# A two-layer hybrid decoder trunk: gate projections placed between attention heads, zero-padded low parts, softmax sums folded into the RMS norm, and scaling moved to ScalarE

## The chip, the cores and the metric

The kernel runs on one core of one Trainium2 chip. The metric is the device time of one execution in microseconds. Smaller is better. Times before and after are medians of several executions; the trace comes from one further execution under the hardware profiler.

## The reference

Two layers, each x <- LayerNorm(alpha * x + f(x)) three times: a hybrid token mixer, a cross-attention into 256 memory tokens, and a dense SwiGLU network. There are 512 tokens of width 1024. The change touches the mixer, cut here to what matters:

```python
def diff_attention(q, k, v, lam, subln_g, lambda_init):        # branch A: 4 heads, 2 softmaxes each
    s = einsum('bqhcd,bkhcd->bhcqk', q, k) * HEAD_DIM ** -0.5
    p = softmax(where(causal, s, -inf))
    w = p[:, :, 0] - lam * p[:, :, 1]
    o = einsum('bhqk,bkhe->bqhe', w, v)
    return rms_norm(o, subln_g) * (1.0 - lambda_init)
...
def rg_lru_branch(xr, gate, ...):                              # branch B: recurrence
    xc = causal_conv(xr)
    gates = einsum('bsnc,gncd->gbsnd', blocks_of_64(xc), gate_w) + gate_b
    ...                                                        # h_t = a_t * h_{t-1} + u_t
    return h * gelu(gate)
...
def hybrid_mixer(x, ...):
    aq, ak, av, rx, rg, cq, ck, cv, gl = split(x @ w_in)
    o_a = diff_attention(rotary(aq), rotary(ak), av, ...)
    o_b = rg_lru_branch(rx, rg, ...)
    o_c = dilated_attention(rotary(cq), rotary(ck), cv)        # branch C: 8 heads, band masks
    g = sigmoid(gl.reshape(B, S, 3, D_MODEL))
    return (g[0] * (o_a @ w_br_a) + g[1] * (o_b @ w_br_b) + g[2] * (o_c @ w_br_c)) @ w_out
```

## The kernel before

All data is float32; every large product is made from a rounded high part and a low remainder (`xh`, `xl` of the activations, `whi`, `wlo` of the weights) as three matmuls: high times high, low times high, high times low. The weights come as 372 chunks of 128 x 1024. A chunk is loaded by a DMA of the SP queue (`raw`), ScalarE casts it to `whi` (line 264), and VectorE subtracts to get `wlo` (line 271); for the chunks in `on_pool` GpSimd subtracts.

`make_program` writes a list of *steps*. A step is one 128 x 512 output in PSUM from eight contraction tiles, hence 24 matmuls (lines 808 to 810, or 837 to 839 where weights are the moving side); steps of the branch projections have half of that. The list's order is the order of the matmuls on TensorE. Before each step the loop at the end of the kernel splits weight chunks ahead (at most `pairs` pairs that have still to be used), issues the work that follows the step before (`POST`), and calls `advance()`. That function moves every running *item* on by one stage and starts one waiting item. An item is a Python generator: `attn_a` and `attn_c` (one head or pair of heads, one block of 128 queries), `rope_item` (the rotary embedding of a projected tile), `b_item` (one tile of 128 channels of the recurrence). What an item issues on TensorE in `advance()` thus stands between two steps, in program order, and a TensorE instruction that has to wait holds up the steps behind it. Every engine works through its instructions in program order.

In branch A a head has a Q tile and a K tile, each one step, followed by `rope_item`: ScalarE copies the PSUM tile, VectorE shuffles it, GpSimd does two multiplications with the tables, VectorE adds (line 572), ScalarE makes the high parts (lines 573 and 574); one advance later VectorE makes the low parts, for Q into the tile `ql` (lines 581 and 582, each twice, so that both halves of the 128 partitions hold both heads' remainders), for K into `qkA` itself (585, 586). `attn_a` then makes scores `sc` (336, 337), a masked minimum on VectorE (346), exponentials on ScalarE with their sums (349), the two weightings (352 to 355), transposes `tp` (360) and the product with V (366), an RMS norm with a power on GpSimd (372), and the output's transpose. `attn_c` is alike, with two heads side by side: the probabilities are scaled by the reciprocal sums on VectorE (398), transposed (404) and multiplied with V (410). In `b_item` the tiles `xs` and `xl` are the high and low parts of the convolved input, `xl` from four subtractions on VectorE (516 and 517); the gate products `z` (521, 522) read them, and ScalarE takes four `tanh` from `z` (524 to 527).

All 128 x 512 tiles in PSUM share eight banks. The tiles of 4 KB per partition, among them `raw`, `whi`, `wlo`, `ql` and `xl`, share a pool of 42 (`a4`). The order in layer 1 is: V of branch A, the Q and K tiles of four heads in a row, V of branch C, the eight gate projections of branch A, the first pair of heads of branch C, and so on. In layer 0 V of branch A stands after the second head.

## Time and profile before

| | before |
|---|---|
| median of 3 runs | 2237.24 us (2236.24 to 2237.97) |
| the profiled execution | 2235.22 us |
| its span, first to last instruction | 2233.4 us |
| TensorE busy (matmuls) | 2180.9 us, 98% |
| VectorE busy | 1318.1 us, 59% |
| ScalarE busy | 893.2 us, 40% |
| GpSimd busy | 300.9 us, 13% |
| mean granted TensorE clock | 0.993 |

The span is what the trace covers; the profiled execution is 1.8 us longer than its span. Busy time of TensorE counts matmuls at whatever clock is granted, so a stretch at half clock is busy and yet slow. The difference of span and TensorE's busy time, 52.5 us, is the time in which TensorE did nothing.

### The profile page before, as it was taken

The page shows a single profiled execution, that of the slowest core. Times are in us where ns is not written, and L with a number is a line of the kernel's source. Part 1 is how long each engine was busy: PE and PEld are TensorE (multiplying, and loading weights), DVE is VectorE, ACT ScalarE, POOL GpSimd, SP SyncE. Part 2 cuts the span into 40 slices and gives each one's busy share as a digit, 9 for nine tenths or more (in the row PEclk, how much of TensorE's full clock was granted, in tenths as well). Part 3 has the DMA queues.
Part 4 walks back from the last instruction along what each step waited for, and adds up shares of the span by engine and source line. Part 5 has one row for each costly group of instructions (what it writes and reads, how often), then busy time and mean ns, then how long its engine had stood idle before and what let it go on. Part 6 is the DMA issues. An engine that isn't in the chain of part 4 may idle for free.

```text
span 2233.4 us, 26831 instructions
## 1 busy us (share of the span) xinstructions
PE 2180.9 (98%) x10516; PEld 1812.8 (81%) x10516; DVE 1318.1 (59%) x2154; ACT 893.2 (40%) x1583; POOL 300.9 (13%) x206
## 2 busy tenths in 40 slices
PE   9999989999999999999998999899999999999998
PEld 7788868888888888888876888688888888888887
DVE  7757767756745743244567577678567457432435
ACT  4454557643333323133134445666433333231330
POOL 2203102210300300000022031022103003000000
PEclk9999999999999999999999999999999999999999
DMA  7122223244333322233221222232334233223321
GB/s 269 49 94 77 93 66 112 84 130 146 123 101 107 105 76 85 92 125 110 88 97 54 77 85 91 67 113 95 125 134 132 95 104 104 85 76 113 105 94 38
DMA packets 65278, 224.37 MB, mean 100 GB/s; under 512 B 7936, under 2 KB 7936, under 8 KB 65152
## 3 DMA queue, kind: packets, MB, share of 16 engines
q1 hardware_dynamic: 65152, 222.66, 30.6%
q8 instruction: 83, 1.36, 0.2%
q14 instruction: 43, 0.35, 0.0%
HBM read 212.14 MB, written 2.10 MB: 96 GB/s over the span
## 4 chain that ended last, share of the span: by engine, by line
PE 69%; issue 17%; DVE 7%; ACT 3%; POOL 3%; DMA 0%; SPq 0%; POOLq 0%; ACTq 0%; DVEq 0%
PE ps L808 17%; PE ps L809 17%; PE ps L810 17%; PE ps L837 5%; PE ps L838 5%; PE ps L839 5%; POOL wlo L271 2%; PE o L410 1%; PE o L366 1%; DVE x L478 1%; POOL ln L473 1%; ACT whi L264 1%; DVE ql L582 1%; DVE xl L516 1%; PE sc L337 1%
## 5 line engine op out<-in xcount | busy, mean ns | idle before, releaser
L808 PE MATMUL ps<-xh,whi 128*128 128x512 f32 (+1 forms) x1792 | 690.5, 385 | 4.2 <-ACT ti L527 2.8
L809 PE MATMUL ps<-xl,whi 128*128 128x512 f32 (+1 forms) x1792 | 688.1, 384 | 1.1 <-DVE xl L752 0.5
L810 PE MATMUL ps<-xh,wlo 128*128 128x512 f32 (+1 forms) x1792 | 687.4, 384 | 1.3 <-POOL wlo L271 1.3
L271 DVE TENSOR_TENSOR wlo<-raw,whi 128x1024 fp32r<-128x1024 f32 x347 | 441.9, 1287 | 40.3 <-ACT whi L264 36.5
L264 ACT CAST whi<-raw 128x1024 fp32r<-128x1024 f32 x371 | 382.0, 1045 | 123.8 <-PE ps L838 61.8
L808 PEld LDWEIGHTS ps<-xh,whi 128*128 128x128 f32 x1792 | 339.0, 189 | 72.4 <-ACT ti L527 4.1
L810 PEld LDWEIGHTS ps<-xh,wlo 128*128 128x128 f32 x1792 | 338.9, 189 | 68.5 <-POOL wlo L271 2.1
L809 PEld LDWEIGHTS ps<-xl,whi 128*128 128x128 f32 x1792 | 339.2, 189 | 66.4 <-DVE xl L867 1.1
L473 POOL TENSOR_TENSOR ln<-ln,expo 128x1 f32<-128x1 f32 x24 | 34.4, 1432 | 1081.3 <-DVE ln L472 1081.3
L837 PE MATMUL ps<-whi,hh 128*128 128x512 f32 x352 | 137.1, 389 | 0.0
L839 PE MATMUL ps<-whi,hl 128*128 128x512 f32 x352 | 137.0, 389 | 0.0
L838 PE MATMUL ps<-wlo,hh 128*128 128x512 f32 x352 | 136.9, 389 | 0.0
L497 ACT CAST xh<-tp 128x256 fp32r<-128x256 f32 x80 | 28.0, 376 | 198.6 <-PE tp L491 121.4
L742 ACT CAST hh<-fg 128x512 fp32r<-128x512 f32 x44 | 27.3, 620 | 191.9 <-DVE fg L741 191.9
L731 DVE SCALAR_TENSOR_TENSOR fg<-fg,ps 128x512 f32<-128x512 f32 x44 | 30.3, 688 | 116.8 <-ACT fg L730 116.8
L741 DVE TENSOR_TENSOR fg<-fg,ps 128x512 f32<-128x512 f32 x44 | 30.2, 687 | 114.4 <-PE ps L810 114.4
L730 ACT ACTIVATE fg<-ps 128x512 f32<-128x512 f32 x44 | 26.3, 598 | 140.7 <-PE ps L810 140.7
L678 DVE SCALAR_TENSOR_TENSOR x<-ps,x 128x512 f32<-128x512 f32 x48 | 32.9, 686 | 80.5 <-PE ps L839 80.4
L839 PEld LDWEIGHTS ps<-whi,hl 128*128 128x128 f32 x352 | 66.1, 188 | 13.7
L838 PEld LDWEIGHTS ps<-wlo,hh 128*128 128x128 f32 x352 | 66.1, 188 | 13.7
L837 PEld LDWEIGHTS ps<-whi,hh 128*128 128x128 f32 x352 | 66.1, 188 | 13.6
L567 POOL TENSOR_TENSOR raw<-raw,tabs 128x512 f32<-128x512 f32 x32 | 42.8, 1339 | 242.5 <-ACT raw L564 242.5
(233 smaller groups left out, 3555.7 us busy)
## 6 DMA issues: line engine op xcount, KB each, us to landing
raw<-in_wts_dram SPq DMA_DIRECT2D x371, 512.0 KB, 3.7
xs<-xs SPq DMA_DIRECT2D x32, 128.0 KB, 2.2
lng<-in_lnp_in_dram SPq DMA_DIRECT2D x6, 512.0 KB, 4.0
lnb<-in_lnp_in_dram SPq DMA_DIRECT2D x6, 512.0 KB, 4.9
tabs<-in_tabs_in_dram SPq DMA_DIRECT2D x4, 512.0 KB, 7.7
x<-in_x_in_dram SPq DMA_DIRECT2D x4, 512.0 KB, 8.5
qkA<-qkA SPq DMA_DIRECT2D x16, 128.0 KB, 2.2
qkC<-qkC SPq DMA_DIRECT2D x16, 128.0 KB, 2.2
```

The costliest lines, as they stand in the source:

```text
L264: A.copy(h, raw)
L271: eng.tensor_tensor(lw, raw, f(h), ALU.subtract)
L473: G.tensor_tensor(st[:, 15:16], st[:, 14:15], expo, ALU.pow)
L567: G.tensor_tensor(raw, raw, tab[:, 0, :], ALU.mult)
L678: V.scalar_tensor_tensor(xs, ps, co, xs, ALU.mult, ALU.add)
L731: V.scalar_tensor_tensor(g, g, 1.0, ps, ALU.add, ALU.mult)
L808: T.matmul(pv, wh, xh, start=(kt == 0), stop=False)
L809: T.matmul(pv, wh, xl, start=False, stop=False)
L810: T.matmul(pv, wl, xh, start=False, stop=(kt == st.nk - 1))
L837: T.matmul(ps, xh, wh, start=(i == 0), stop=False)
L838: T.matmul(ps, xh, wl, start=False, stop=False)
L839: T.matmul(ps, xl, wh, start=False, stop=(i == n - 1))
```

## The change

Five edits. (1) In `make_program` the gate projections of branch A move: in layer 0 from behind V of branch C to places behind the second, third and fourth head (two, three, three), in layer 1 two behind every head; V of branch C follows them. `pairs` of the heads falls from 6 to 5 or 4, that of V of branch C from 6 to 5. (2) `ql` and `xl` are no longer allocated. Three fixed tiles `pad` are zeroed once by GpSimd and used in turn; only the half that carries a head's (or block's) own remainder is written, and the other half stays zero. So two subtractions stand where four did; in `b_item` one of the two goes to GpSimd. The pool `a4` has 39 tiles in place of 42. (3) In `attn_a` the first softmax is not divided by its sum: the second is scaled by -lambda times the ratio of the sums, one full-width multiplication goes, and the square of the first sum times the epsilon takes the epsilon's place in the RMS norm. (4) In `attn_c` the two scalings by reciprocal sums move from VectorE to ScalarE. (5) The first two chunks of the memory's key projection leave `on_pool`, so VectorE makes their low parts.

```diff
+NPAD = 3
...
-        def a_heads(h0, h1):
-            for h in range(h0, h1):
-                tile_step("w_in", l, OFF_AQ + P * h, "x", ("rope", l, "A", h, 0), pairs=6)
-                tile_step("w_in", l, OFF_AK + P * h, "x", ("rope", l, "A", h, 1), pairs=6)
-
-        if l == 0:
-            a_heads(0, 2)
-            group("w_in", l, 0, KT, OFF_AV, "x", ("v", l, "A"), 6)
-            a_heads(2, 4)
-        else:
-            group("w_in", l, 0, KT, OFF_AV, "x", ("v", l, "A"), 6,
-                  needs=("x%d_3_{t}" % (l - 1),), pre=("tabs",))
-            a_heads(0, 4)
+        def a_head(h, pairs):
+            tile_step("w_in", l, OFF_AQ + P * h, "x", ("rope", l, "A", h, 0), pairs=pairs)
+            tile_step("w_in", l, OFF_AK + P * h, "x", ("rope", l, "A", h, 1), pairs=pairs)
...
-        group("w_in", l, 0, KT, OFF_CV, "x", ("v", l, "C"), 6)
-        gates("A", *range(KT))
+        if l == 0:
+            a_head(0, 6)
+            a_head(1, 6)
+            group("w_in", l, 0, KT, OFF_AV, "x", ("v", l, "A"), 6)
+            gates("A", 0, 1)
+            a_head(2, 4)
+            gates("A", 2, 3, 4)
+            a_head(3, 4)
+            gates("A", 5, 6, 7)
+        else:
+            group("w_in", l, 0, KT, OFF_AV, "x", ("v", l, "A"), 6,
+                  needs=("x%d_3_{t}" % (l - 1),), pre=("tabs",))
+            for h in range(4):
+                a_head(h, 5 if h < 2 else 4)
+                gates("A", 2 * h, 2 * h + 1)
+        group("w_in", l, 0, KT, OFF_CV, "x", ("v", l, "C"), 5)
...
-        return big.tile([P] + shape, dt, tag="a4", name=nm(s), bufs=42)
+        return big.tile([P] + shape, dt, tag="a4", name=nm(s), bufs=39)
...
+    pads = [cp.tile([P, 2, S], F32R, tag="pad%d" % k, name="pad%d" % k) for k in range(NPAD)]
+    turn = [0]
+
+    def padded():
+
+        turn[0] += 1
+        return pads[turn[0] % NPAD]
...
-               if (name == "xkv" and c0 < D) or (name == "w_up" and c0 % HID < 2 * P)}
+               if (name == "xkv" and 2 * P <= c0 < D) or (name == "w_up" and c0 % HID < 2 * P)}
...
-        V.reciprocal(st[:, 4:6], st[:, 2:4])
-        V.tensor_scalar(st[:, 6:7], st[:, 5:6], neglam[:, l:l + 1], None, ALU.mult)
-        V.tensor_scalar(pr[0][:, :w], pr[0][:, :w], st[:, 4:5], None, ALU.mult)
+        V.reciprocal(st[:, 4:5], st[:, 3:4])
+        V.scalar_tensor_tensor(st[:, 6:7], st[:, 2:3], neglam[:, l:l + 1], st[:, 4:5], ALU.mult, ALU.mult)
         V.scalar_tensor_tensor(pr[0][:, :w], pr[1][:, :w], st[:, 6:7], pr[0][:, :w],
                                ALU.mult, ALU.add)
+        V.tensor_scalar(st[:, 5:6], st[:, 2:3], st[:, 2:3], LN_EPS, ALU.mult, ALU.mult)
...
-        V.tensor_scalar(st[:, 8:9], st[:, 7:8], LN_EPS, None, ALU.add)
+        V.tensor_tensor(st[:, 8:9], st[:, 7:8], st[:, 5:6], ALU.add)
...
-            V.tensor_scalar(pr[c][:, :w], pr[c][:, :w], st[:, 4 + c:5 + c], None, ALU.mult)
+            A.activation(pr[c][:, :w], pr[c][:, :w], AF.Copy, scale=st[:, 4 + c:5 + c])
...
-        xl = a4("xl", [2, S], F32R)
-        for r in (u, w):
-            V.tensor_tensor(xl[r, 0, :], xc[u], f(xs[u, 0, :]), ALU.subtract)
-            V.tensor_tensor(xl[r, 1, :], xc[w], f(xs[w, 1, :]), ALU.subtract)
+        xl = padded()
+        G.tensor_tensor(xl[u, 0, :], xc[u], f(xs[u, 0, :]), ALU.subtract)
+        V.tensor_tensor(xl[w, 1, :], xc[w], f(xs[w, 1, :]), ALU.subtract)
...
-            ql = a4("ql", [2, S], F32R)
-            for w in (a, b):
-                V.tensor_tensor(ql[w, 0, :], raw[a], f(st[a, 0, :]), ALU.subtract)
-                V.tensor_tensor(ql[w, 1, :], raw[b], f(st[b, 1, :]), ALU.subtract)
+            ql = padded()
+            V.tensor_tensor(ql[a, 0, :], raw[a], f(st[a, 0, :]), ALU.subtract)
+            V.tensor_tensor(ql[b, 1, :], raw[b], f(st[b, 1, :]), ALU.subtract)
...
+    for pd in pads:
+        G.memset(f(pd[64:P, 0, :]), 0.0)
+        G.memset(f(pd[0:64, 1, :]), 0.0)
     make_identity(nc, ident)
```

How instructions stand on three engines before and now. First VectorE in the branch-A heads of layer 1: before, from the Q tile of head 2 on (`ql` is the low part, `sc` the scores of head 0's first query block, `sh` the shuffle of a projected tile; the pair 581, 582 stands twice):

```order
L565 STREAM_SHUFFLE sh_9161<-ps_9129 128x512
L581 TENSOR_TENSOR ql_9168<-raw_9065,qkA_9125 64x512
L582 TENSOR_TENSOR ql_9168<-raw_9065,qkA_9125 64x512
...
L572 TENSOR_TENSOR raw_9113<-raw_9113,sh_9114 128x512
L346 ISA pr_9178,st_9177<-sc_9180,tabs_8779 128x128
...
L271 TENSOR_TENSOR wlo_9158<-raw_9060,whi_9157 128x1024
L565 STREAM_SHUFFLE sh_9222<-ps_9190 128x512
L585 TENSOR_TENSOR qkA_9173<-raw_9113,qkA_9173 64x512
L586 TENSOR_TENSOR qkA_9173<-raw_9113,qkA_9173 64x512
L352 RECIPROCAL st_9177<-st_9177 128x2
```

The same place now, from the low part of head 0's Q tile to the weighting of its first block; `sh_9091` belongs to head 1:

```order
L592 TENSOR_TENSOR pad_80<-raw_8939,qkA_8985 64x512
L593 TENSOR_TENSOR pad_80<-raw_8939,qkA_8985 64x512
L584 TENSOR_TENSOR raw_8979<-raw_8979,sh_8980 128x512
L596 TENSOR_TENSOR qkA_9023<-raw_8979,qkA_9023 64x512
L597 TENSOR_TENSOR qkA_9023<-raw_8979,qkA_9023 64x512
L577 STREAM_SHUFFLE sh_9091<-ps_9059 128x512
L359 ISA pr_9097,st_9096<-sc_9099,tabs_8740 128x128
...
L284 TENSOR_TENSOR wlo_9085<-raw_8972,whi_9084 128x1024
```

Before, the first scores of head 0 stand behind the low parts of head 1's Q tile, while the tiles of head 2 already come out; now they stand behind the shuffle of head 1's Q tile, and no other head's low parts lie between.

Second, ScalarE where the first gate products `z` of the recurrence meet the last head pairs of branch C. Before (`gq` is the GELU of the gate, `tr` and `ti` the four `tanh` of `z`):

```order
L405 COPY wT_2636<-tp_2641 128x256
L661 ACTIVATE gq_2550<-gq_2550 128x512
L393 ACTIVATE pr_2659,st_2658<-pr_2659,st_2658 128x512
L393 ACTIVATE pr_2660,st_2658<-pr_2660,st_2658 128x512
L264 CAST whi_2699<-raw_2545 128x1024
L414 CAST oCh_1797<-o_2707 128x128
L524 ACTIVATE tr_2720<-z_561_2714,hb 64x512
```

Now:

```order
L418 COPY wT_2621<-tp_2626 128x256
L411 ACTIVATE pr_2565<-pr_2565,st_2564 128x384
L411 ACTIVATE pr_2566<-pr_2566,st_2564 128x384
L672 ACTIVATE gq_2535<-gq_2535 128x512
L406 ACTIVATE pr_2641,st_2640<-pr_2641,st_2640 128x512
L406 ACTIVATE pr_2642,st_2640<-pr_2642,st_2640 128x512
L277 CAST whi_2681<-raw_2530 128x1024
L427 CAST oCh_1791<-o_2689 128x128
L536 ACTIVATE tr_2702<-z_552_2696,hb 64x512
```

The two scalings by the reciprocal sums (line 411) have come in ahead of the GELU's `tanh`; the order of the rest is the same.

Third, GpSimd in the last blocks of the recurrence in layer 0. Now (`acc` is the merge of branch C, `bl` the low part of branch B's output, `pad` the low part of a convolved tile):

```order
L559 TENSOR_TENSOR ti_3646<-ti_3646,m_3518 128x512
L640 TENSOR_TENSOR acc_2213<-acc_2213,g_3594 128x512 x2
L569 TENSOR_TENSOR bl_3337<-m_3518,bh_3336 128x512 x2
L528 TENSOR_TENSOR pad_79<-xc_3803,xs_3868 64x512
L559 TENSOR_TENSOR ti_3817<-ti_3817,m_3862 128x512
```

Before, the same five places held the same instructions without the fourth: a low part that VectorE made is now queued on GpSimd behind two merges and two subtractions. On TensorE the instructions between the steps stand as before, item by item; only the steps that they stand between have changed places.

## Rows read from the trace of the kernel before

**Rows 1.** The page: busy time by engine; weight loads (KB, us to landing).

```profile
PE 2180.9 (98%) x10516; PEld 1812.8 (81%) x10516; DVE 1318.1 (59%) x2154; ACT 893.2 (40%) x1583; POOL 300.9 (13%) x206
...
raw<-in_wts_dram SPq DMA_DIRECT2D x371, 512.0 KB, 3.7
```

**Rows 2.** Waits of TensorE over the whole span: total us, times, longest.

```profile
PE tp L360 <- DVE pr L355: 14.3, 6, 5.6
PE sc L336 <- ACT ti L525: 7.1, 4, 2.9
...
PE ps L808 <- ACT ti L527: 2.8, 4, 0.7
PE tp L404 <- DVE st L390: 2.4, 2, 1.2
PE z L522 <- DVE xl L516: 1.6, 2, 0.8
```

**Rows 3.** Busy time in stretches: length, then PE, PEld, DVE, ACT, POOL, clock.

```profile
40.00:60.00 20.00, 20.00 (x90) 16.57 (x89) 12.41 (x15) 10.01 (x14) 2.98 (x2) 1.00 0.53 171
60.00:100.00 40.00, 35.92 (x170) 30.01 (x168) 32.90 (x66) 16.47 (x39) 13.92 (x10) 0.96 0.14 40
280.00:340.00 60.00, 53.79 (x277) 41.75 (x276) 39.00 (x83) 36.37 (x76) 2.91 (x2) 0.94 0.26 73
1160.00:1220.00 60.00, 47.83 (x215) 38.85 (x214) 45.93 (x92) 24.92 (x57) 17.75 (x13) 0.94 0.17 49
1400.00:1440.00 40.00, 33.80 (x173) 25.98 (x172) 28.80 (x62) 22.92 (x49) 1.54 (x1) 0.91 0.23 67
```

**Rows 4.** Stretches with a lower granted clock: length, PE busy, clock.

```profile
90.00:94.00 4.00, 3.50 (x12) 0.57 0.20 48
294.00:304.00 10.00, 6.99 (x20) 0.66 0.00 0
1182.00:1190.00 8.00, 5.91 (x16) 0.57 0.42 115
1408.00:1416.00 8.00, 5.07 (x14) 0.57 0.01 2
```

**Rows 5.** Groups by line: busy us, mean ns, idle time ahead.

```profile
L271 DVE TENSOR_TENSOR wlo<-raw,whi 128x1024 fp32r<-128x1024 f32 x347 | 441.9, 1287 | 40.3 <-ACT whi L264 36.5 <-PE ps L838 3.7
...
L398 DVE TENSOR_SCALAR pr<-pr,st 128x128 f32<-128x128 f32 (+3 forms) x64 | 32.5, 550 | 1.1
...
L516 DVE TENSOR_TENSOR xl<-xc,xs 64x512 fp32r<-64x512 f32 x32 | 27.7, 865 | 0.6 <-ACT xs L509 0.3
...
L405 ACT COPY wT<-tp 128x128 f32<-128x128 f32 (+3 forms) x64 | 24.1, 430 | 1.8 <-PE tp L404 1.7
...
L582 DVE TENSOR_TENSOR ql<-raw,qkA 64x512 fp32r<-64x512 f32 x16 | 15.0, 937 | 0.2
...
L354 DVE TENSOR_SCALAR pr<-pr,st 128x128 f32<-128x128 f32 (+3 forms) x32 | 14.0, 437 | 0.0
...
L772 POOL TENSOR_TENSOR gw<-gr,gw 64x512 fp32r<-64x512 f32 x8 | 11.2, 1404 | 40.9 <-ACT gw L770 40.4
```

**Rows 6.** VectorE at the first gate products of layer 0, in time order.

```profile
284.95 1.52 DVE L516 TENSOR_TENSOR xl<-xc,xs 64x512 fp32r<-64x512 f32 x1
286.49 1.69 DVE L517 TENSOR_TENSOR xl<-xc,xs 64x512 fp32r<-64x512 f32 x1
...
289.83 0.75 DVE L398 TENSOR_SCALAR pr<-pr,st 128x384 f32<-128x384 f32 x2
```

**Rows 7.** ScalarE in the same stretch.

```profile
291.67 0.63 ACT L661 ACTIVATE gq<-gq 128x512 f32<-128x512 f32 x1 [6.41 <-DVE gq L660]
```

**Rows 8.** ScalarE in branch A of layer 1.

```profile
1184.72 0.62 ACT L573 CAST qkA<-raw 64x512 fp32r<-64x512 f32 x1 [5.26 <-DVE raw L572]
```

**Rows 9.** GpSimd at the last gate products of layer 0.

```profile
447.42 3.42 POOL L557 TENSOR_TENSOR bl<-m,bh 128x512 fp32r<-128x512 f32 x2
```

**Rows 10.** TensorE at the same place.

```profile
451.45 0.50 PE L522 MATMUL z<-xl,gw 128*128 128x512 f32 x1 [0.80 <-DVE xl L516]
```

## The prediction

> **What bounds the kernel now.** I read the busy line of the page first: TensorE is busy for 2180.9 of the 2233.4 us of the span, the others for 59% and less [rows 1]. The order lists show TensorE's instructions unchanged, with steps that have changed places, so the change can take away or add only two things: time in which TensorE stands still, 2233.4 - 2180.9 = 52.5 us in all, and time in which it works at a lower clock. Whether VectorE or ScalarE gets lighter counts only where TensorE waits for it.
>
> The waits of TensorE over the whole span say where [rows 2]. The transposes `tp` of branch A wait for VectorE's weighting `pr`, 14.3 us in six waits. Scores `sc` and step outputs `ps` wait for a `tanh` that ScalarE reads out of `z`, 7.1 and 2.8 us: not for its data, but for the PSUM bank that `z` holds. Transposes of branch C wait 2.4 us for a maximum in `st`, and `z` waits 1.6 us for `xl`.
>
> Four stretches hold nearly all of this. Length less PE busy [rows 3]: the A heads of layer 0, 40.00 - 35.92 = 4.08 us; the A heads of layer 1, 60.00 - 47.83 = 12.17; the place where the recurrence's first gate products meet branch C, 60.00 - 53.79 = 6.21 in layer 0 and 40.00 - 33.80 = 6.20 in layer 1. Together 28.66 us. An undisturbed stretch beside them has 90 matmuls in 20.00 us, no idle time and clock 1.00, so 0.222 us a matmul and 5.33 us a step of 24.
>
> Each of the four is followed by a piece at a low granted clock, the lower of the levels 1.2 and 2.4 GHz in part of it [rows 4]. Work at clock c costs (1 - c) of its busy time: 3.50 x 0.43 = 1.5 us, 6.99 x 0.34 = 2.4, 5.91 x 0.43 = 2.5, 5.07 x 0.43 = 2.2, together 8.6. In each, TensorE had stood still before the clock fell.
>
> **The change part by part.** *Gates between heads, half the `ql` work, one weighting fewer* (edits 1, 2, 3). In layer 1, eight rope steps stand in a row. VectorE is busy for 45.93 of 60 us there [rows 3], and the ping-pong between engines adds to it: ScalarE stands 5.26 us for a VectorE sum before it can make a high part [rows 8]. The sequence falls 12.17 us behind over four heads, 3.0 each. Per head the change removes two `ql` subtractions of 0.94, 1.9 us, and one weighting of 0.44 per block, 4 x 0.44 = 1.8, against small one-column operations that I take at 0.2 per block, so 0.8 [rows 5]; net 2.9, nearly the shortfall. Two gate steps per head then give 2 x 5.33 = 10.7 us of TensorE's work that asks of VectorE only two `wlo` of 1.29, so 8.1 us in which it catches up. 2.9 + 8.1 is well over 3.0. In layer 0 the shortfall is 4.08 and there are two or three gates to a head. So I take these waits as gone: 4.08 + 12.17 = 16.25, and their clock losses 1.5 + 2.5 = 4.0; 20.3 us in all. From below: if a wait is pure latency, the gates don't help unless they stand between a block's scores and its transposes; items advance one stage per step, so they do stand there.
>
> *Half the `xl` work, scalings on ScalarE* (edits 2, 4). At the junction VectorE makes four `xl`, from 284.95 on, the first two at 1.52 and 1.69 us, then scales `pr` twice, 0.75 [rows 6]. ScalarE meanwhile waits 6.41 us for the VectorE product behind them, `gq` [rows 7], and its `tanh`, which free the banks, come late. Now VectorE has one `xl` of some 1.7 and no scaling, so ScalarE goes on some 3.6 us earlier; the scalings fill time in which it stood still. TensorE loses its 1.2 us wait for `st` and so reaches the scores 1.2 earlier; of the longest bank wait of 2.9 there remains 2.9 + 1.2 - 3.6 = 0.5. The bank wait of a step, 0.7, and some 1.3 at the next block stay: 2.5 us in each layer, 5.0 together, of 6.21 + 6.20 = 12.41. With no wait over a microsecond the clock should hold, which gives 2.4 + 2.2 = 4.6. Gain 12.41 - 5.0 + 4.6 = 12.0.
>
> *Half of `xl` on GpSimd* (edit 2). The nearest row, GpSimd on 64x512, has 1.40 us, VectorE's `xl` 0.87 [rows 5]. At the last gate products of layer 0 GpSimd makes `bl` from 447.42 to 450.84 [rows 9], and the new half stands behind it: done at 450.84 + 1.4 = 452.2. `z` started at 451.45 after 0.80 of waiting [rows 10], so it may be up to 0.8 late. I take the waits for `xl`, 1.6, as unchanged. For this choice of engine the Trainium skill, GPSIMD Engine Reference, section 4.1 (Engine selection), recommends VectorE for elementwise work on a tile and gives GpSimd as about two times slower for two inputs. Our rows, 1.40 against 0.87, agree in direction; by the page's ratio the half would take an estimated 1.7, and end 0.3 later. What that would do at every block is a rival below.
>
> *At nothing.* ScalarE's 64 scalings: between 0.43, the copy of `wT`, and 0.63, the `gq` of 128x512 [rows 5, 7], so 27.5 to 40 us on an engine that is 40% busy; hidden by its waits, except at the junction, where two at 0.63 would give back 1.3 per layer, or 2.6. Edit 5 gives VectorE four `wlo` more (two per layer), 4 x 1.29 = 5.2 us; no wait for VectorE among the large ones [rows 2] lies at that projection, so work of steps without a wait covers them, and without that cover they cost at most those 5.2. The pool of 39 for 42: `ql` and `xl`, up to two or three at a time, no longer draw on it; a chunk needs 3.7 us to land [rows 1], a cast, and 1.29 for `wlo`, some 6 us, and the pairs ahead reach over at least two steps, over 10 us. If it did not suffice in one group, a chunk's `wlo` would be late by one 1.29. The pads are zeroed in six instructions of at most 1.4 us, 8.4 us on a GpSimd with little to do at the start; a reader of a pad is done over a step before its next writer, since three take turns. If two blocks overlapped, a write would wait for a product of some microseconds, on VectorE's queue, with `wlo` behind it.
>
> **Sum.** 20.3 + 12.0 = 32.3 us. The profiled execution took 2235.22, so 2202.9 after; the median is 2.02 higher than it, so 2205 us.
>
> **The rivals.** *B, the junction stays as it is*: ScalarE's new scalings and the wait for GpSimd eat what VectorE saves, because the banks are freed by `tanh` that stand behind more ScalarE work (the order lists show the two scalings ahead of the `tanh`). Only 20.3 are gained: 2217 us. For it speaks that ScalarE is the releaser there; against it, that it stood 6.41 us for VectorE.
>
> *C, all waits go*: bank waits and clock losses vanish whole, and `xl` is early, 28.66 + 8.6 + 1.6 = 38.9: 2198 us.
>
> *D, slower: the GpSimd half is late at every block.* There are 16 blocks. If each `z` waits for a GpSimd that is held up by a pair as in rows 9, 3.42 us each, 16 x 3.42 = 54.7 is lost and 32.3 gained: 2205 + 55 = 2260 us. It decides from 32.3 / 16 = 2.0 us a block. The section named above speaks for it in kind. Against it, GpSimd is busy 13% of the span [rows 1], and the one place that I find with such a queue ahead costs at most 0.8.
>
> *E, the A waits move*: with the gates spent between the heads, V of branch C and the first C pair follow without cover, with `pairs` 5 and tiles fewer; the chunks of that V group come late or C's first transposes wait, as A's did. Of A's 20.3 us all is lost again: 2225 us. For it speaks that C's rope steps carry the same VectorE work; against it, that C's low parts now cost half.
>
> **How the numbers follow.** Forecast 0.58, B 0.17, C 0.10, E 0.08, D 0.07. The prediction is the forecast's 2205. The range reaches down to C, with 2 us for waits elsewhere that a lighter VectorE may end, 2196, and up to B with E's half (2217 + 4), 2221; beyond lie D, E, and a little of C, under 2 in 10. A measurement of this kernel can tell about 0.2%, 4.5 us, from no change. Faster by more: the forecast, B, C and nearly all of E, 0.90. Within: E with a junction that gains nothing, 0.04. Slower: most of D, 0.06.
>
> **What would show it.** Right: the waits of `tp` for the weighting in the A heads are gone or under 1 us; granted clock 1.00 in the A heads of both layers and at the junctions; `sc` waits under 1 us for `tanh`; TensorE's idle time 52.5 - 16.25 - (12.41 - 5.0) = 28.8 us; VectorE's busy time lower by 32 `ql` x 0.94 = 30, 48 `xl` x 0.87 = 42, 32.5 and 14.0 [rows 5], 118 less the small operations and edit 5, so some 105 us; ScalarE's higher by 27 to 40, GpSimd's by 16 x 1.4 = 22 less what edit 5 takes away. Wrong: `z` waiting for `pad` from GpSimd at many blocks (D), a wait of `ps` for `wlo` in V of branch C (E), or bank waits as long as before with ScalarE never idle before the `tanh` (B).

## The result and the profile after

The changed kernel takes 2210.5 us (median of four runs, 2209.66 to 2210.88), the kernel before 2237.6 in the same comparison (2236.24 to 2241.66). The ratio is 0.9875, interval 0.9858 to 0.9892: faster by 1.25%, or 27 us by the medians, where the prediction had 32. The profiled execution took 2210.49 us, 24.7 less than the profiled one of before.

The page's busy line, to be held against the first of [rows 1]:

```profile
PE 2176.0 (99%) x10516; PEld 1811.4 (82%) x10516; DVE 1228.7 (56%) x2014; ACT 925.4 (42%) x1647; POOL 316.1 (14%) x224
```

The span is 2208.7 us. TensorE's idle time fell from 52.5 to 2208.7 - 2176.0 = 32.7 us, by 19.8, and its busy time, which holds the work at half clock (the lower of the two levels, 1.2 of 2.4 GHz), by 4.9. The prediction had 28.8 us of idle time. VectorE lost 89.4 us of work (105 forecast), ScalarE gained 32.2 (27 to 40) and GpSimd 15.2.

The waits of TensorE over the whole span (total, times, longest), which answer to [rows 2]:

```profile
PE ps L821 <- POOL wlo L284: 5.1, 6, 1.9
PE z L534 <- POOL pad L528: 4.4, 2, 2.2
PE ps L819 <- ACT ti L539: 3.3, 4, 1.0
...
PE sc L349 <- ACT ti L537: 0.7, 2, 0.4
...
PE ot L390 <- DVE st L365: 0.6, 1, 0.6
...
PE tp L373 <- DVE pr L367: 0.2, 1, 0.2
```

The transposes' wait for the weighting has gone from 14.3 us to 0.2, the scores' wait for a bank from 7.1 to 0.7. The waits of `ps` for a bank are slightly longer (2.8 before, 3.3). New at this size is `z` waiting for GpSimd's `pad`, 4.4 us in two waits, where 1.6 went to VectorE's `xl`. The wait for GpSimd's `wlo` is not new: it was 5.0 us before, and by its size it now stands first.

The same stretches as in [rows 3] (length; PE, PEld, DVE, ACT, POOL busy; granted clock). The junction of layer 1 now begins before 1400, so its row starts at 1380; 140 to 160 is where the last A heads of layer 0 end:

```profile
60.00:100.00 40.00, 40.00 (x199) 33.70 (x198) 24.42 (x65) 19.90 (x51) 7.58 (x7) 1.00 0.18 60
140.00:160.00 20.00, 18.98 (x102) 15.75 (x101) 11.20 (x51) 8.92 (x28) 1.66 (x4) 1.00 0.00 1
280.00:340.00 60.00, 57.86 (x315) 45.96 (x314) 35.43 (x69) 45.76 (x88) 9.25 (x7) 1.00 0.25 81
1160.00:1220.00 60.00, 60.00 (x305) 50.85 (x304) 45.13 (x111) 33.06 (x87) 17.02 (x16) 1.00 0.22 71
1380.00:1440.00 60.00, 57.86 (x315) 46.06 (x314) 33.86 (x64) 47.13 (x90) 5.62 (x4) 1.00 0.23 71
```

In layer 1's A heads TensorE now runs 60.00 of 60 us, at full clock, with VectorE as busy as before (45.13 against 45.93): 305 matmuls fit where 215 did, and VectorE's work per matmul is what fell. Each junction keeps 60.00 - 57.86 = 2.14 us of waits.

ScalarE at the junction of layer 0, which answers to [rows 7]:

```profile
281.40 1.13 ACT L411 ACTIVATE pr<-pr,st 128x384 f32<-128x384 f32 x2 [1.49 <-DVE st L409]
283.31 0.64 ACT L672 ACTIVATE gq<-gq 128x512 f32<-128x512 f32 x1 [0.78 <-DVE gq L671]
```

It waits 1.49 + 0.78 us for VectorE where it waited 6.41; the two scalings lie in the time that came free.

GpSimd, TensorE and VectorE at the last gate products of layer 0, which answer to [rows 9, 10]:

```profile
436.38 3.17 POOL L569 TENSOR_TENSOR bl<-m,bh 128x512 fp32r<-128x512 f32 x2
439.52 2.24 POOL L528 TENSOR_TENSOR pad<-xc,xs 64x512 fp32r<-64x512 f32 x1
```

```profile
441.82 0.50 PE L534 MATMUL z<-pad,gw 128*128 128x512 f32 x1 [2.21 <-POOL pad L528]
```

```profile
435.30 1.67 DVE L529 TENSOR_TENSOR pad<-xc,xs 64x512 fp32r<-64x512 f32 x1
...
439.04 1.60 DVE L284 TENSOR_TENSOR wlo<-raw,whi 128x1024 fp32r<-128x1024 f32 x1
```

VectorE's half was done at 435.30 + 1.67 = 436.97. GpSimd's stood behind the pair `bl` and then took 2.24 us (the median of its sixteen is 1.31), beside a VectorE `wlo` that took 1.60 (its mean is 1.285 in this trace). TensorE was kept 2.21 us.

Last, the clock behind waits of about 2 us. First two short stretches of the changed kernel, the wait for the fourth key chunk of the memory and what follows, and then, by 20 us, the four places where its clock falls: behind the `z` wait and the key chunk of layer 0, and behind both in layer 1 (two rows and one). Below them stand the key chunk's stretches in the kernel before:

```profile
578.00:582.00 4.00, 2.13 (x18) 1.92 (x17) 3.56 (x2) 0.00 (x0) 4.00 (x3) 1.00 0.79 297
582.00:586.00 4.00, 4.00 (x23) 4.00 (x22) 1.74 (x5) 2.86 (x6) 3.29 (x2) 0.57 0.47 135
```

```profile
440.00:460.00 20.00, 18.18 (x73) 14.88 (x74) 7.91 (x8) 10.11 (x14) 1.77 (x1) 0.91 0.30 98
580.00:600.00 20.00, 18.80 (x144) 18.76 (x145) 13.88 (x22) 13.10 (x26) 11.60 (x5) 0.91 0.41 131
1520.00:1540.00 20.00, 17.79 (x75) 14.35 (x74) 17.23 (x18) 12.12 (x19) 8.32 (x5) 0.95 0.42 149
1540.00:1560.00 20.00, 20.00 (x87) 16.42 (x85) 5.07 (x5) 10.55 (x13) 0.83 (x1) 0.96 0.20 71
1660.00:1680.00 20.00, 18.12 (x103) 16.04 (x102) 17.37 (x23) 1.90 (x5) 10.40 (x6) 0.95 0.51 184
```

```profile
586.00:590.00 4.00, 2.12 (x18) 1.92 (x17) 3.56 (x2) 0.00 (x0) 4.00 (x3) 1.00 0.92 355
590.00:594.00 4.00, 4.00 (x36) 4.00 (x35) 2.00 (x5) 2.60 (x5) 3.31 (x2) 1.00 0.70 185
```

The wait for the key chunk is the same in both (1.87 us of idle in four, 18 matmuls). Before, full clock follows and 36 matmuls fit into the next 4 us; after, the clock falls to its lower level for most of them and 23 fit. A fall's cost is estimated as the busy time times what the granted clock lacks of 1.00: 1.6 us at 440, 1.7 at 580, 0.9 + 0.8 at 1520 and 1540, 0.9 at 1660 and 0.6 in the 20 us after it (20.00 busy at 0.97). So each costs 1.5 to 1.7 us, and the four, 6.5 us together, are new: the kernel before has full clock behind these waits.

### The profile page after: what moved, and what is told of

It is laid out like the page before. It is cut to its first block, busy times and chain, and to the rows that moved or that the text cites. A ratio compares the mean times of both kernels' runs of the same rounds, so it can differ in the third digit from the quotient of the medians.

```text
span 2208.7 us, 26772 instructions
## 1 busy us (share of the span) xinstructions
PE 2176.0 (99%) x10516; PEld 1811.4 (82%) x10516; DVE 1228.7 (56%) x2014; ACT 925.4 (42%) x1647; POOL 316.1 (14%) x224
## 4 chain that ended last, share of the span: by engine, by line
PE 67%; issue 22%; DVE 5%; POOL 4%; ACT 2%; DMA 0%; POOLq 0%; SPq 0%; ACTq 0%
PE ps L819 16%; PE ps L820 16%; PE ps L821 16%; PE ps L848 5%; PE ps L850 5%; PE ps L849 5%; POOL wlo L284 2%; PE o L423 1%; PE tp L417 1%; POOL ln L486 1%; PE sc L350 1%; PE sc L349 1%; DVE x L491 1%; PE o L379 1%; POOL bl L569 1%
```

## The experiments

Every kernel was timed in the same comparison with the kernel before (2236.2 to 2237.8 us). "Waits" are TensorE's idle time in the stretches named.

| kernel | median us (range) | ratio to before, interval |
|---|---|---|
| the changed kernel | 2210.5 (2209.66 to 2210.88) | 0.9875, 0.9858 to 0.9892 |
| 1: `xl` on VectorE | 2203.7 (2203.49 to 2205.41) | 0.9856, 0.9842 to 0.9869 |
| 2: order alone | 2226.2 (2223.98 to 2226.62) | 0.9953, 0.9941 to 0.9966 |
| 3: all but the order | 2223.9 (2221.38 to 2224.90) | 0.9943, 0.9930 to 0.9955 |
| 4: scalings on VectorE | 2215.8 (2212.45 to 2217.69) | 0.9906, 0.9891 to 0.9921 |
| 5: without edit 5 | 2209.8 (2208.49 to 2210.06) | 0.9880, 0.9866 to 0.9893 |
| 6: two repairs, on VectorE | 2208.5 (2207.60 to 2209.10) | 0.9875, 0.9861 to 0.9888 |
| 7: without edit 3 | 2209.2 (2208.91 to 2210.30) | 0.9879, 0.9865 to 0.9892 |
| 8: `ql` made twice | 2220.6 (2218.96 to 2224.66) | 0.9931, 0.9917 to 0.9944 |
| 9: last `xl` on VectorE | 2200.3 (2199.95 to 2204.76) | 0.9837, 0.9824 to 0.9851 |
| 10: the same, key chunks earlier | 2194.4 (2194.31 to 2197.17) | 0.9810, 0.9796 to 0.9823 |
| 11: all `xl` on GpSimd | 2211.2 (2210.86 to 2211.87) | 0.9882, 0.9869 to 0.9896 |
| 12: order and `ql` | 2218.1 (2216.92 to 2218.91) | 0.9912, 0.9899 to 0.9926 |

### The A heads: order or fewer operations (2, 3, 12, 8, 7)

Experiment 2 is the kernel before with edit 1 alone:

```diff
-        group("w_in", l, 0, KT, OFF_CV, "x", ("v", l, "C"), 6)
-        gates("A", *range(KT))
...
+            for h in range(4):
+                a_head(h, 5 if h < 2 else 4)
+                gates("A", 2 * h, 2 * h + 1)
+        group("w_in", l, 0, KT, OFF_CV, "x", ("v", l, "C"), 5)
```

> The kernel before with edit 1 alone (gate projections between the heads, the new `pairs`); ql, xl, the weighting, the scalings and the pool as before. Theory: two gate steps between heads are cover enough for VectorE's backlog, so the waits of the A heads (16.3 us) and their clock loss (4.0) go by the order alone, and the junctions keep theirs: 2237.6 - 20.3 = 2217 us. Rival: the fewer VectorE operations did it; then the order alone removes half of the waits or less, and the time is 2227 us or more.

It took 2226.2 us, 10 better than before: nearly the rival. The stretch 60 to 100 and that from 1160 to 1220 are clean, but TensorE now waits later, at the end of the heads:

```profile
140.00:160.00 20.00, 16.38 (x72) 13.40 (x72) 13.45 (x56) 8.07 (x26) 1.82 (x3) 0.83 0.00 0
...
1220.00:1260.00 40.00, 36.47 (x181) 29.69 (x181) 30.54 (x79) 21.84 (x59) 8.91 (x9) 1.00 0.14 46
```

3.62 + 3.53 = 7.15 us idle, and 16.38 x 0.17 = 2.8 us of half clock behind the first. The gates moved the place of the shortfall and halved it.

Experiment 3 is the changed kernel with the old order in `make_program`:

```diff
-            for h in range(4):
-                a_head(h, 5 if h < 2 else 4)
-                gates("A", 2 * h, 2 * h + 1)
-        group("w_in", l, 0, KT, OFF_CV, "x", ("v", l, "C"), 5)
...
+        group("w_in", l, 0, KT, OFF_CV, "x", ("v", l, "C"), 6)
+        gates("A", *range(KT))
```

> The changed kernel with edit 1 undone (edits 2 to 5 alone). By the prediction's working the fewer VectorE operations save 2.9 us a head of a shortfall of 3.0 us, so little is left for the order: the waits of the A heads come back by 3 us or less, 2211 to 2214 us. Rival: the waits are the ping-pong between engines, which fewer subtractions do not shorten; then the order does nearly all, the waits come back by 10 us or more with their clock loss, and the time is 2222 to 2231 us.

2223.9 us: the rival. The A heads by the windows of this kernel:

```profile
60.00:100.00 40.00, 37.04 (x176) 30.73 (x175) 30.48 (x65) 19.50 (x49) 13.48 (x10) 0.96 0.18 53
...
1160.00:1220.00 60.00, 52.95 (x242) 44.06 (x242) 41.34 (x95) 29.17 (x73) 15.59 (x13) 0.91 0.21 67
```

2.96 + 7.05 = 10.0 us of the 16.25 are still there, with a granted clock of 0.91 over the sixty microseconds of layer 1. So neither part does it alone. Experiment 12 puts the order and the halved `ql` together (the kernel before with edit 1, the three zeroed tiles, the pool of 39, and):

```diff
-            ql = a4("ql", [2, S], F32R)
-            for w in (a, b):
-                V.tensor_tensor(ql[w, 0, :], raw[a], f(st[a, 0, :]), ALU.subtract)
-                V.tensor_tensor(ql[w, 1, :], raw[b], f(st[b, 1, :]), ALU.subtract)
+            ql = padded()
+            V.tensor_tensor(ql[a, 0, :], raw[a], f(st[a, 0, :]), ALU.subtract)
+            V.tensor_tensor(ql[b, 1, :], raw[b], f(st[b, 1, :]), ALU.subtract)
```

> The kernel before with edit 1 and the `ql` part of edit 2 (fixed tiles, two subtractions, pool of 39); xl, the weighting, the scalings and the key chunks as before. Theory: order and the halved `ql` together make the whole gain of the A heads, of which each alone made half: their waits fall under 2 us and their half clock goes, the junctions keep 12 us of waits: 2214 to 2219 us. Rival: the weighting and the lighter VectorE in general are needed too; 4 us or more of waits stay in the A heads, 2221 us or more.

2218.1 us, as the theory had it. In its trace the A heads keep 1.75 us (140 to 160) and 1.01 us (1220 to 1260) at full clock, 2.76 together, a little over the theory's 2 and under the rival's 4; the scores' waits for a bank stay at 7.0 us in total. Experiment 8 is the reverse test, the changed kernel with the two subtractions repeated:

```diff
-            V.tensor_tensor(ql[a, 0, :], raw[a], f(st[a, 0, :]), ALU.subtract)
-            V.tensor_tensor(ql[b, 1, :], raw[b], f(st[b, 1, :]), ALU.subtract)
+            for _ in range(2):
+                V.tensor_tensor(ql[a, 0, :], raw[a], f(st[a, 0, :]), ALU.subtract)
+                V.tensor_tensor(ql[b, 1, :], raw[b], f(st[b, 1, :]), ALU.subtract)
```

> The changed kernel with each of the two `ql` subtractions made twice, so that VectorE has the four of before (into the fixed tiles). Theory: the order alone left 7 us of waits in the A heads and the fewer operations alone 10 us, so the two are needed together, and of the operations the `ql` pair (1.4 us on VectorE just ahead of the sum that ScalarE waits for) is the larger: 2 to 7 us of waits come back, with a half clock behind a long one: 2213 to 2220 us. Rival: the gates cover it; 2210 to 2212 us.

2220.6 us: 10 us lost for 32 subtractions of 0.68 us, just past the theory's upper end. By its waits, `ot` stands 2.7 us for a value of VectorE's `st` where it stood 0.6, and the scores wait 2.8 us for a bank where they waited 0.7:

```profile
PE sc L349 <- ACT ti L537: 2.8, 2, 1.4
PE ot L390 <- DVE st L365: 2.7, 1, 2.7
```

The scores' waits are at the junctions: branch C's Q tiles carry the same pair, and some 4 of the 10 us are lost there (1.06 and 1.05 us of idle time, 1.6 of half clock). The repeated pair makes VectorE's load greater and its chain longer at once, so this run does not tell the two apart. Experiment 7 undoes edit 3:

```diff
-        V.reciprocal(st[:, 4:5], st[:, 3:4])
-        V.scalar_tensor_tensor(st[:, 6:7], st[:, 2:3], neglam[:, l:l + 1], st[:, 4:5], ALU.mult, ALU.mult)
+        V.reciprocal(st[:, 4:6], st[:, 2:4])
+        V.tensor_scalar(st[:, 6:7], st[:, 5:6], neglam[:, l:l + 1], None, ALU.mult)
+        V.tensor_scalar(pr[0][:, :w], pr[0][:, :w], st[:, 4:5], None, ALU.mult)
...
-        V.tensor_scalar(st[:, 5:6], st[:, 2:3], st[:, 2:3], LN_EPS, ALU.mult, ALU.mult)
...
-        V.tensor_tensor(st[:, 8:9], st[:, 7:8], st[:, 5:6], ALU.add)
+        V.tensor_scalar(st[:, 8:9], st[:, 7:8], LN_EPS, None, ALU.add)
```

> The changed kernel with edit 3 undone (the first softmax is divided by its sum again, one more full-width product and no small ones). The product stands directly ahead of the weighting for which the transposes waited. Theory: with gates between the heads VectorE is ahead by several microseconds a head, so 0.8 us a head is covered; within 1 us of the changed kernel, 2209.5 to 2211.5 us. Rival: the waits of the A heads hang on the latency of one chain rather than on VectorE's load, so a product of 0.44 us in the chain shows in each block that is close to its limit; waits of 1 to 3 us come back in the A heads: 2212 to 2216 us.

2209.2 us, 0.3 under the theory's range and within the play of the changed kernel, whose range it overlaps. The waits for the weighting are 1.2 us where they were 0.2, `ot`'s 1.1 where they were 0.6; that microsecond and a half is less than what the clock's falls make of a kernel (below). Edit 3 is worth nothing that these runs can tell, and VectorE's rows say why: its busy time is 1231.8 us here and 1228.7 with the edit. The product that went is paid for by one-column operations that came. In each of the 32 blocks of the changed kernel the ratio of the sums takes 0.50 us and the epsilon 0.21 (first two rows); without the edit the one-column operation in the ratio's place takes 0.21, here and in the kernel before (last row), and there is none for the epsilon:

```profile
L366 DVE SCALAR_TENSOR_TENSOR st<-st,neglam 128x1 f32<-128x1 f32 x32 | 15.9, 498 | 1.1
L369 DVE TENSOR_SCALAR st<-st 128x1 f32<-128x1 f32 x32 | 6.6, 207 | 0.0
```

```profile
L353 DVE TENSOR_SCALAR st<-st,neglam 128x1 f32<-128x1 f32 x32 | 6.8, 214 | 1.1
```

### The junction: scalings and `xl` (4, 1)

```diff
-            A.activation(pr[c][:, :w], pr[c][:, :w], AF.Copy, scale=st[:, 4 + c:5 + c])
+            V.tensor_scalar(pr[c][:, :w], pr[c][:, :w], st[:, 4 + c:5 + c], None, ALU.mult)
```

> The changed kernel with edit 4 undone (the 64 scalings by reciprocal sums on VectorE again). Theory of the prediction: at each junction VectorE is longer by two scalings of 0.75 us, ScalarE's product `gq` comes that much later and so do the tanh that free the banks; waits of 1 to 3 us in each layer come back: 2212 to 2216 us. Rival: what the junction gained came from the shorter `xl` alone, and ScalarE had room neither way; within 1 us of the changed kernel, 2209.5 to 2211.5 us.

2215.8 us, 5.3 more than the changed kernel: the theory. The two junctions:

```profile
280.00:340.00 60.00, 56.16 (x300) 44.40 (x299) 39.61 (x77) 37.90 (x74) 9.54 (x6) 0.97 0.25 77
1380.00:1440.00 60.00, 56.16 (x301) 44.36 (x299) 39.65 (x78) 39.30 (x75) 8.15 (x5) 0.97 0.23 72
```

3.84 us idle in each instead of 2.14, and the clock falls in both. Against the 6.2 us of before, the shorter `xl` alone is thus worth 2.4 us in each junction, the scalings' move 1.7 and the half clock that does not follow. Experiment 1 moves GpSimd's half of `xl` to VectorE:

```diff
-        G.tensor_tensor(xl[u, 0, :], xc[u], f(xs[u, 0, :]), ALU.subtract)
+        V.tensor_tensor(xl[u, 0, :], xc[u], f(xs[u, 0, :]), ALU.subtract)
```

> The changed kernel, with GpSimd's half of `xl` made by VectorE (two subtractions there, none on GpSimd). Theory: the waits of `z` for `pad`, 2.2 us at the last block of each layer, are GpSimd's queue, and the lower clock behind them (1.6 us of work in layer 0, 1.7 in layer 1) is their consequence; both go, 2.8 to 4.4 + 3.3 us, and the time falls from 2210.5 to 2203 to 2205 us. Rival: the second subtraction on VectorE, 0.7 to 1.7 us, makes the tanh at the junctions late again, the bank waits come back by 1 to 2 us in each layer with a lower clock behind them, and the time is 2209 or more.

2203.7 us, the theory, though the rival's mechanism is there too. No wait of `z` is left among the listed ones; the scores wait 2.3 us for their banks (0.7 before this edit), the junctions have 2.91 and 2.76 us idle, and the clock falls behind one of them:

```profile
280.00:340.00 60.00, 57.09 (x312) 45.32 (x311) 36.56 (x72) 44.75 (x89) 5.09 (x4) 1.00 0.28 84
1380.00:1440.00 60.00, 57.24 (x297) 45.74 (x298) 33.69 (x65) 45.76 (x86) 2.54 (x2) 0.97 0.22 70
```

GpSimd's half is thus, by the waits, a gain at the first block and a loss at the last. At the first its queue is not empty either (two `gw` end at 282.27 in the changed kernel), but the half is done at 283.71, and `z` reads it from 285.81 on.

### GpSimd's queue (11, 9, 6, 10)

Experiment 11 puts both halves of `xl` on GpSimd at every block:

```diff
-        V.tensor_tensor(xl[w, 1, :], xc[w], f(xs[w, 1, :]), ALU.subtract)
+        G.tensor_tensor(xl[w, 1, :], xc[w], f(xs[w, 1, :]), ALU.subtract)
```

> The changed kernel with both halves of `xl` on GpSimd: the prediction's rival D put to the test by doubling its cost, 1.3 us more of GpSimd ahead of every `z`. If GpSimd is near its limit at every block (D), 16 times 1.3 us or more comes on, 2230 us and up. If only the last block of a layer has a queue ahead of it, as the trace of the changed kernel has it, two waits grow by 1.3 us each and VectorE's lighter junction gives a little back: 2211 to 2216 us.

2211.2 us: rival D is dead as a rule for all blocks. The waits of `z` rise by 1.7 us in all, to 5.5 in two waits and 0.6 in a third; the other blocks hide twice the work. The time rises by 0.7 only; in its profile no half clock follows the key chunk's waits. Experiment 9 leaves GpSimd its half except at the last block:

```diff
-        G.tensor_tensor(xl[u, 0, :], xc[u], f(xs[u, 0, :]), ALU.subtract)
+        (V if n == KT - 1 else G).tensor_tensor(xl[u, 0, :], xc[u], f(xs[u, 0, :]), ALU.subtract)
```

> The changed kernel, with VectorE making both halves of `xl` at the last block of each layer alone. The runs so far showed that a wait of 1.9 to 2.2 us is followed by half clock in some profiles and not in others, 1.6 us each time, so the sum has that play. Theory: the waits of `z` (4.4 us) go with what half clock follows them (3.3 us in the changed kernel's profile), and the junctions keep GpSimd's half, so their bank waits do not grow by the 1.4 us that VectorE's half cost there: 2201 to 2204 us. Rival: the better junction is lost in the clock's play and the kernel is no faster than with both halves on VectorE everywhere (2203.7).

2200.3 us, 0.7 under the theory's lower end and 10 us less than the changed kernel for two instructions moved. Two waits of 2.2 us are gone, and in its profile three of the four falls of the clock: both behind `z`, 3.3 us, and that behind the key chunk of layer 0, 1.7 us, whose wait the edit does not touch (1.88 us as before). The last two runs go after the wait for the fourth key chunk. In GpSimd's queue this `wlo` stands behind the last of four powers of the LayerNorm, each of which waits for VectorE. Experiment 6 is experiment 9 with the first five key chunks on VectorE:

```diff
-               if (name == "xkv" and 2 * P <= c0 < D) or (name == "w_up" and c0 % HID < 2 * P)}
+               if (name == "xkv" and 5 * P <= c0 < D) or (name == "w_up" and c0 % HID < 2 * P)}
```

> The changed kernel with two repairs: at the last block of each layer VectorE makes both halves of `xl` (GpSimd at the other seven), and the first five key chunks of the memory are VectorE's instead of the first two. Theory: the waits of `z` (4.4 us) and for the fourth key chunk (3.7 us) are GpSimd's queue, behind two merges and two low parts here and behind three powers of the LayerNorm there; with them goes the half clock behind each, 1.6 us in four places. 2210.5 - 4.4 - 3.7 - 6.5 = 2196 us, and the junctions stay as good as with GpSimd's half; 2195 to 2199. Rival: VectorE stands in the same LayerNorm chain at the key chunks, so that wait stays and with it its clock; 2201 to 2203 us.

2208.5 us: worse than both theories. The wait grew from 1.9 to 4.4 us:

```profile
PE ps L821 <- DVE wlo L284: 8.8, 2, 4.4
```

VectorE's queue at this place shows why:

```profile
575.18 1.28 DVE L491 SCALAR_TENSOR_TENSOR x<-x,ln,lnb 128x1024 f32<-128x1024 f32 x1 [0.44 <-POOL ln L486]
...
577.24 0.76 DVE L511 TENSOR_TENSOR xl<-tp,xh 128x256 fp32r<-128x256 f32 x2 [0.44 <-ACT xh L510]
...
578.77 4.54 DVE L284 TENSOR_TENSOR wlo<-raw,whi 128x1024 fp32r<-128x1024 f32 x2
```

The chunk's `wlo` now stands behind the same LayerNorm and the low parts of the transposed tile besides. By this, what is late is the place in the program and not the engine. Experiment 10 therefore is experiment 9 with chunks split further ahead:

```diff
         for h in range(2):
-            group("w_out", l, 0, KT, 512 * h, "m", ("ln", l, 1, h), 5,
+            group("w_out", l, 0, KT, 512 * h, "m", ("ln", l, 1, h), 5 + 2 * h,
```

> The same, and the second half of the output projection splits up to seven chunk pairs ahead instead of five, so that two key chunks of the memory stand ahead of the LayerNorm's powers in GpSimd's queue instead of behind the last of them. Theory: the waits of 1.87 us in both layers were that order alone; they go, with the half clock behind them where there was one: 3.7 to 7 us less than without it, 2195 to 2199 us. Rival: the powers stand behind 2.7 us of low parts now, the LayerNorm of the next tile comes later, and TensorE waits for its transposes instead: no gain or a loss, 2201 to 2206 us.

2194.4 us, just under the theory's lower end and the fastest kernel of the study, 16 us below the changed kernel and 43 below the kernel before. GpSimd's queue in its trace, and TensorE around the two places:

```profile
558.80 1.52 POOL L486 TENSOR_TENSOR ln<-ln,expo 128x1 f32<-128x1 f32 x1 [85.58 <-DVE ln L485]
560.30 5.73 POOL L284 TENSOR_TENSOR wlo<-raw,whi 128x1024 fp32r<-128x1024 f32 x2
565.98 1.53 POOL L486 TENSOR_TENSOR ln<-ln,expo 128x1 f32<-128x1 f32 x1
```

```profile
430.00:450.00 20.00, 20.00 (x90) 16.56 (x89) 16.59 (x18) 13.04 (x20) 6.36 (x4) 1.00 0.43 145
550.00:590.00 40.00, 40.00 (x248) 35.98 (x247) 29.73 (x38) 8.74 (x16) 22.23 (x10) 1.00 0.40 143
```

Two `wlo` now stand behind the first power, and the second power has no wait for VectorE ahead of it any more: VectorE's value was ready at 565.53, and the power starts 0.45 us later. Its tile has slack, and TensorE does not stand still.

### Edit 5 and the clock (5)

```diff
-               if (name == "xkv" and 2 * P <= c0 < D) or (name == "w_up" and c0 % HID < 2 * P)}
+               if (name == "xkv" and c0 < D) or (name == "w_up" and c0 % HID < 2 * P)}
```

> The changed kernel with edit 5 undone (all eight key chunks of the memory on GpSimd again). Before and with the order alone, the wait of 1.87 us for the fourth key chunk was followed by full clock; in the four other kernels, which all have edit 5, by half clock (1.6 us of work lost, in both layers). If edit 5 causes that, the clock stays at 1.00 behind this wait in both layers and the time falls by some 3 us, 2207 to 2208 us, unless the chunks bring a wait of their own. Rival: the pieces only fall differently in time, and edit 5 does nothing; the clock falls there as before this edit was undone and the time stays at 2210 to 2211 us.

2209.8 us, within the changed kernel's range: the rival. In this profile the clock fell behind the key chunk's wait in layer 0 and stayed in layer 1, so the fall does not need edit 5. Over all profiles that have the wait, 1.83 to 1.88 us twice in each, half clock followed in 14 of 24 (never before, nor in experiments 2 and 11; always in the changed kernel and experiments 1, 3, 4 and 8; in experiments 5, 7, 9 and 12 in one layer and not in the other). Behind the wait of 2.2 us for `pad` it followed in 9 of 12.

## Why the prediction came out as it did

The time, 2210.5 us, lies within the range and 5.5 us above the value. The waits that were to go went, for the reasons given; one term was put too low (the last gate products), and 6.5 us of new half clock stand nowhere in the working. That the range holds this loss is luck: it reached so far up for rivals B and E, which did not come. By its own terms, in the profiled executions:

**The A heads, 20.3 us: right as a size.** 16.25 us of waits became none in the two stretches and 1.02 at 140 to 160, and their half clock is gone. The working behind it held one wrong step. It put the saving of VectorE's work at 2.9 us a head, "nearly the shortfall", and the gates' room at 8.1 us, so that either should have nearly done it. Experiments 2 and 3 show that each alone does about half (7.15 and 10.0 us of 16.25 remain), and 12 that order and `ql` together do nearly all of it. The room of 8.1 us counts VectorE's free time. In experiment 2 VectorE is busy for only 13.45 of 20 and 30.54 of 40 us in the stretches where TensorE still waits for it; this points to the length of one chain per head rather than to VectorE's load, but no run separates the two (8 lengthens both). The weighting, 1.8 us a head less 0.8 for small operations in the working, has no measurable worth (7): the small operations were taken at 0.2 us a block and cost 0.5, which eats the saving and is most of what VectorE's busy time fell short of the 105 us.

**The junction, 12.0 us: right, a little small.** 12.41 us of waits became 4.28 (the prediction had 5.0), and 4.6 us of half clock went. Both parts matter: without the scalings' move 5.3 us come back, and the shorter `xl` keeps 2.4 us of each junction (4). Of rival B's objection, that ScalarE's extra work delays the `tanh`, nothing is seen: the steps' waits for a bank are 3.3 us against 2.8 before, but they are 3.3 with the scalings on VectorE too (4).

**The last gate products: the term that was mis-sized.** "I take the waits for `xl`, 1.6, as unchanged." They are 4.4. The order of GpSimd's queue was read rightly, the pair `bl` and then the new half, and so was the end of the half, 452.2, up to 0.8 us behind the start of `z`; but this 0.8 a layer did not enter the sum. The rest is the half itself, which took 2.24 us beside a VectorE `wlo` and not the 1.4 of the row that was chosen. TensorE did not come earlier against the queue: it stood ready at 441.82 - 2.21 = 439.61, 0.06 us behind the end of `bl`, where before it was 0.19 ahead (450.65 and 450.84 by [rows 9, 10]). Over both layers that is 2.8 us, and the clock behind both waits took 3.3 more in this profile. In experiment 9 the whole 4.4 us and the 3.3 are gone; the rest of its 9.0 us between the profiled executions is about what the fall behind the key chunk of layer 0 had cost. The Trainium skill, GPSIMD Engine Reference, section 4.1 (Engine selection), gives GpSimd as about two times slower for two inputs. The trace agrees in direction, and in size by the subtraction of the same shape in the rope steps: a mean of 1.50 us on GpSimd (median 1.31) and 0.69 on VectorE. Against VectorE's own half of `xl`, 1.12, it is 1.3 times:

```profile
L528 POOL TENSOR_TENSOR pad<-xc,xs 64x512 fp32r<-64x512 f32 x16 | 24.0, 1499 | 134.4 <-ACT xs L522 134.4
```

```profile
L529 DVE TENSOR_TENSOR pad<-xc,xs 64x512 fp32r<-64x512 f32 x16 | 17.9, 1120 | 3.4 <-ACT xs L523 3.2
...
L593 DVE TENSOR_TENSOR pad<-raw,qkA 64x512 fp32r<-64x512 f32 x8 | 5.5, 690 | 0.2
```

Yet the slower engine is the better one at the first block (9 against 1: the scores wait 0.7 us for their banks and not 2.3; the ranges of the two times overlap) and indifferent at most others (11).

**The clock, 8.6 us: gone where predicted, back elsewhere.** The four stretches of [rows 4] have full clock. But 6.5 us of half clock stand behind waits that cost nothing in clock before, the two for the key chunk, and behind the two grown ones. The prediction took "no wait over a microsecond" as the condition; idle time of 1.0 us at 140 to 160, in three waits of which the longest is 0.7, was also followed by half clock in three of eight profiles (experiments 5, 10 and 11). Whether a given wait of 1 to 2 us is followed by half clock differs from kernel to kernel, and from layer to layer of one kernel, with the same pieces around it. The Trainium skill, TensorE: Matmul & The Clock Gate, Part 1, says that the monitor behind the clock runs free of the program, so that the same code can meet it at another phase; the 14 of 24 agree with that, though no run here shows the phase itself.

The sum: 32.3 forecast, less 1.0 at 140 to 160, 2.8 at `z`, 6.5 of new half clock and 0.5 at the start (4.2 us idle in the first 20 us and not 3.7; in all profiles with the zeroed tiles it is 3.5 to 4.2, so this is play), and with 0.7 more at the junction: 22.2, against 24.7 measured by the profiled executions. The idle time in this sum comes out, 20.1 against 19.8; the 2.5 us lie in TensorE's busy time, 8.6 - 6.5 = 2.1 in the sum and 4.9 measured. By 20 us stretches the four old falls cost 9.3 us and not 8.6, which is some of it. The rest is not assigned to a place; the granted clock of a stretch is a mean and its cost an estimate.

**The rivals.** C (all waits gone, 2198) has nearly the time that experiment 9 reached with two instructions moved, and 10 went below it by a wait that was there before the change; but not C's way, for in both the waits for banks stay (0.7 and 3.3 us). D holds at the last block alone. E's new cover problem was not seen: from 1220 to 1260 the changed kernel waits 0.17 us. With VectorE's full `ql` work a wait of 0.6 us for a `wlo` does stand there (experiments 2 and 8). A pool of 39, the zeroed tiles and edit 5 cost nothing that the trace or experiment 5 can tell.

## What to carry to other kernels

Where TensorE is 98% busy, list its waits by stretch with the granted clock behind each, and price each with its clock; a shortfall of one stretch often needs both more cover and less work, and halving either alone may only move it. When work goes to an engine that is mostly idle, look at what stands ahead of it in that engine's queue at each of its places, not at its busy share: 14% busy, and yet late at two of sixteen places. A full-width operation traded for several one-column ones may gain nothing: price the small ones from rows. A chunk that came late behind a chain was mended by its place in the program; another engine stood in the same chain.

## What the runs showed of the hardware that was not expected

A wait of TensorE of 1.87 us was followed by full clock (36 matmuls in the next 4 us) or by the lower level (23) with the same instructions around it, in 10 and 14 of 24 cases; each fall in the changed kernel cost 1.5 to 1.7 us. Timed runs of one kernel spread by 1.2 us (the changed kernel) to 7.1 (the kernel before, timed with experiments 9 to 12). The mean granted clock of each timed run is on record, and much of the spread goes with it: in experiment 8 0.994 at 2219.0 us and 0.991 at 2224.7, in that of the kernel before 0.993 at 2235.5 and 0.989 at 2242.5. Not all of it: in experiment 2 the fastest run, 2224.0 us, has 0.992 and the slowest, 2226.6, has 0.995.

GpSimd and VectorE took longer side by side: GpSimd's 64x512 subtraction 2.24 us beside a VectorE `wlo`, against a median of 1.31, and that `wlo` 1.60, where those with no GpSimd product or subtraction beside them took 1.21. Not every pair does so: beside VectorE's own half of `xl`, at 367.23, GpSimd's half took 1.28; in experiment 6 two `wlo` on VectorE took 4.54 us together, beside three on GpSimd.
